# Delta-rule recurrence of a hybrid backbone: Gram products in two halves, the triangular solve woven as a generator

## The chip, the cores and the metric

The kernel runs on one core of one Trainium2 chip. The metric is device time in microseconds (us) of one launch that computes both layers; lower is better. Matrix work is on PE (TensorE; its weight loads are the row PEld), element-wise work on DVE (VectorE) and ACT (ScalarE), small copies on POOL (GpSimd), and SP issues the loads of weights.

## What is computed

The model has two layers over a trunk of 256 context and 512 latent tokens of width 1024. Each layer projects its normed input into three branches (a bidirectional RWKV-7 recurrence, a convolution of 31 taps, grouped-query attention), merges them with gates, and runs a squared-ReLU MLP. The change lies in the recurrence alone, 16 heads of 64 channels, once forward and once in reverse:

```
    def step(S, inp):
        r_t, w_t, k_t, v_t, kk_t, a_t = inp
        s_kk = jnp.einsum('bhij,bhj->bhi', S, kk_t)
        S = (S * w_t[:, :, None, :]
             - s_kk[..., None] * (kk_t * a_t)[:, :, None, :]
             + v_t[..., None] * k_t[:, :, None, :])
        return S, jnp.einsum('bhij,bhj->bhi', S, r_t)
```

The last layer gives out latent tokens only, so that its reads `r` of the context's four chunks of 64 tokens are not needed.

## The kernel before

The recurrence is computed in chunks of 64 tokens, 12 chunks to the 768 tokens, and in pairs of heads: one head lies on partitions 0 to 63, the other on 64 to 127 (`ROWS[0]`, `ROWS[1]`). Eight pairs follow each other in a layer. For one pair the work is, in the order of its data:

- **prep**: the rows `k`, `r`, `v` of the pair come out of the projection; `rw_kk` norms `kk`; `rw_decay` makes the running sums `sg` of the log decay (both directions); `rw_keys` writes `BK`, for each chunk the 128 columns that hold the decayed key and the decayed `kk*a`.
- **grams** (`rw_front`): `KR` takes `kk` (slot 0) and `r` (slot 1), each times the exponential of `sg`. For each of 12 chunks, 2 heads and 2 directions one fp32 matmul has `BK` as stationary operand (64 rows by 128 columns) and both slots of `KR` as moving operand (128 columns; 64 where the last layer needs no `r`). It is issued as two pairs of weight load and matmul in the profile. DVE masks the results into `GL` and `GB`; `GB` takes transposes of `BK` too.
- **seeds and solve** (`rw_seed`, `rw_solve`): DVE inverts the 32x32 triangular blocks of `GL` in some 60 dependent steps between transposes. `rw_rest` meanwhile makes `KM` from `GL`, `UV` and transposes of `KR` slot 0.
- **merge and batch** (`rw_merge`, `rw_batch`): the blocks are joined to 64x64 inverses, and applied.
- **chain** (`rw_chain`): 12 steps, each needs the state `S` of the step before it; it reads `KR`, `GB` and `UV`. Then `rw_readout`.

Beside this run **jobs**: the 128-column slices of the big input projection (line 412), that is `k`, `r` and `v` of the next pair, the convolution's two inputs, and the columns of attention and gates ("spills"). A slice is eight jobs, one for each 128 rows of the contraction, and a job is six matmuls of 384 columns (three of 512 for slices that need latent tokens alone). The 31 **taps** of the convolution run on DVE.

`weave` advances several generators in turn; each yields an estimate in us, and `pe` puts out that many times `ratio` jobs, so that the jobs fill TensorE between the small matmuls. In the kernel before, the loop over pairs weaves merge, batch and chain of pair p with prep and grams of pair p+1 (the grams in three parts, behind `wait('s3')`, `wait('s7')`, `wait('s11')`, which are steps of the chain). Behind that stand `rw_solve`, `rest` and `s.fill(F['solve'])`, 26 jobs in the first layer and 34 in the second. The framework then orders each engine's instructions itself by its own estimate; taps and a few matmuls are pinned. PSUM tiles of the small products come from a pool of two banks (`s.g`).

Of the kernel before, what the change touches and what calls it, by code (L numbers as in the profile page):

```python
# [47 lines left out]
SCHED = [dict(open=1.3, first=0.55, mid=0.5, end=0.4, solve=26, early=4, tap0=1, tap1=1, merge=1.2, sums=0, grams=0, rest=9, ln=9, pad=1, last=1.15, tap2=1),  # L48
         dict(open=1.2, first=0.4, mid=0.4, end=0.4, solve=34, early=5, tap0=0.8, tap1=0.8, merge=1.4, sums=0, grams=0, rest=9, ln=9, pad=1, last=0.85, tap2=1.1)]
# [27 lines left out]
class Kern:  # L77
# [364 lines left out]
    def conv_jobs(s, l, P, j, T, dst):  # L442
# [8 lines left out]
        def done_b(ps):  # L451
            hold['c'] = s.rp.tile([128, L], F32, tag="cv", name="cv")
            nc.scalar.activation(out=s.dv0(hold['c'], T), in_=s.pv(ps, T), func=AF.Tanh, scale=0.5)
# [313 lines left out]
    def rw_keys(s, P, p, I, Q, d):  # L767
# [22 lines left out]
        if d:  # L790
            Q['key', 1] = key
        yield 0.2

    def rw_front(s, I, Q, d, g, lat):

        nc = s.nc
        c = slice(4 * g, 4 * g + 4)
        n = 1 if lat and g == 0 else 2
        sg = s.c64(Q['sg', d])[:, c]
        KR, BK, GL, GB = (s.big[x, d] for x in ('KR', 'BK', 'GL', 'GB'))  # L800

        nc.gpsimd.memset(KR[:, 0, c, 63 * d:63 * d + 1], 1.0)
        nc.scalar.activation(out=KR[:, 0, c, 1 - d:64 - d], in_=sg[:, :, d:63 + d], func=AF.Exp, scale=CDEC)
        nc.scalar.activation(out=KR[:, 1, c], in_=sg, func=AF.Exp, scale=CDEC)
        if ('lam', d) not in Q:
            Q['lam', d] = s.rt("lam%d" % d, [128, 12], 2)
        nc.gpsimd.tensor_copy(Q['lam', d][:, c], KR[:, 1, c, 63 * (1 - d)])
        nc.vector.tensor_tensor(out=KR[:, 0, c], in0=s.c64(I['kk'])[:, c], in1=KR[:, 0, c], op=ALU.mult)  # L808
        if n == 2:
            nc.vector.tensor_tensor(out=KR[:, 1, c], in0=s.c64(I['r'])[:, c], in1=KR[:, 1, c], op=ALU.mult)  # L810
        yield 0.3
        gp = [s.g([128, 4, 2, 64]) for h in range(2)]
        for q in range(4):
            for h in range(2):
                nc.tensor.matmul(gp[h][:, q, 0:n, :], lhsT=BK[ROWS[h], 4 * g + q].rearrange("p a b -> p (a b)"),  # L815
                                 rhs=KR[ROWS[h], 0:n, 4 * g + q, :], start=True, stop=True)
        for h in range(2):
            for x, G in ((0, GL[:, h, c]), (1, GB[:, h, c, 1]))[:n]:
                nc.vector.tensor_tensor(out=G, in0=gp[h][:, :, x, :],
                                        in1=s.mask(d, h, x).unsqueeze(1).to_broadcast([128, 4, 64]), op=ALU.mult)  # L820
        yield 1.0
        bk = s.g([128, 4, 2, 64])
        for q in range(4):
            nc.tensor.transpose(out=bk[:, q].rearrange("p a b -> p (a b)"), in_=BK[:, 4 * g + q].rearrange("p a b -> p (a b)"), identity=s.ident)  # L824
        nc.scalar.activation(out=GB[:, :, c, 0, :], in_=bk.rearrange("p c h j -> p h c j"), func=AF.Copy)
        yield 0.45
# [14 lines left out]
    def rw_rest(s, d):  # L841

        nc = s.nc
        KR, GL, UV, KM = (s.big[x, d] for x in ('KR', 'GL', 'UV', 'KM'))
# [8 lines left out]
        for h in range(2):  # L853
            s.rw_transpose(KR[:, 0].rearrange("p c t -> p (c t)"), h, lambda par: KM[ROWS[h], par::2, 0, :])
            yield 0.35

    def rw_solve(s):
# [5 lines left out]
        for k in range(1, 31):  # L863
# [3 lines left out]
            nc.vector.tensor_tensor(out=X[:, k + 1:, 0:k], in0=X[:, k + 1:, 0:k], in1=tm, op=ALU.add)  # L867
        nc.vector.transpose(out=s.Z[:, 0:1024].rearrange("p (u c) -> p c u", c=32), in_=X.rearrange("p a b -> p b a"))
        nc.vector.transpose(out=s.Z[:, 768:1792].rearrange("p (u t) -> p t u", t=32), in_=X)

    def rw_bonus(s, P, p, I, Q, T):
# [3 lines left out]
        nc.vector.tensor_tensor(out=ks[:, o:], in0=ks[:, o:], in1=Q['key', 1][:, o:], op=ALU.add)  # L875
        nc.vector.scalar_tensor_tensor(out=ks[:, o:], in0=I['r'][:, o:], scalar=P['v']('rw_r_k')[:, p:p + 1], in1=ks[:, o:], op0=ALU.mult, op1=ALU.mult)
        yield 0.1
# [261 lines left out]
    def rwkv_phase(s, l, P, T):  # L1139
# [3 lines left out]
        with ExitStack() as rc:  # L1143
# [31 lines left out]
            def prep(p, I, Q, wait, *held):  # L1175

                return chain(s.after(I, 'k', 0, s.rw_kk(P, p, I)), *held, s.rw_decay(P, p, Q), wait('b0'), s.rw_keys(P, p, I, Q, 0), wait('b1'), s.rw_keys(P, p, I, Q, 1),
                             s.after(I, 'r', 0, s.rw_bonus(P, p, I, Q, T)))

            def grams(I, Q, part):  # L1180

                a, b = ((0, 0), (1, 2), (2, 1))[part]
                c = [slice(0, 8), slice(8, 12)] if part == 1 else [slice(0, 4), slice(8, 12)]
                gs = [s.rw_front(I, Q, 0, a, lat), s.rw_front(I, Q, 1, b, lat)]
                if part == 1:
                    gs.append(s.rw_seed(0, slice(0, 8)))
                if part == 2:
                    gs += [s.rw_seed(1, slice(0, 12)), s.rw_seed(0, slice(8, 12))]
                return chain(*gs)

            def rest(I):
                return chain(s.rw_values(I), s.rw_rest(0), s.rw_rest(1))
            I, In = {}, {}
            s.rw_inputs(l, P, 0, T, I, 'krv')
            s.fill(24)
            Q = s.rw_open(l, 0)
            spills(F['early'])
# [261 lines left out]
```

## Time and profile before

| | |
|---|---|
| median of three runs | 4373.38 us (4372.7 to 4377.01) |
| profiled execution, its own time | 4372.14 us |
| its span, first to last instruction | 4370.4 us |
| mean granted TensorE clock | 0.963 |
| PE busy / PEld busy | 95% / 78% of the span |
| DVE / ACT / POOL busy | 62% / 42% / 7% |
| recurrence of layer 0 / layer 1, steady part | 190 to 1290 us / 2600 to 3540 us |

The span is the time between the first and the last instruction that the trace holds; the execution's own time lies 1.7 us above it, and the median of the three runs 1.2 us above that. Ends of matmuls in the trace are modelled, so that a PE that is shown busy may still be slowed from inside: how long a matmul takes of the engine's time is read from the start of one to the start of what follows it.

### The profile page before, as it was taken

What the parts mean: (1) busy time and instruction counts of PE and PEld (TensorE: products, weight loads), DVE (VectorE), ACT (ScalarE), POOL (GpSimd) and SP (SyncE); (2) the same over time, 40 slices, a digit from 0 to 9 for tenths busy, and PEclk for the clock granted to TensorE, in tenths of its full rate; (3) what the DMA queues carried; (4) which work ended last, traced back from release to release, by engine and by line L of the source; (5) the groups of instructions that cost most, each with busy time, mean ns of one, the idle gap of its engine ahead of it and who ended that gap; (6) DMA issues with size and microseconds to landing.
All of it is one profiled execution on the core that took longest, in us unless ns stands there. A gap on an engine that the chain in (4) does not pass through costs nothing.

```text
span 4370.4 us, 77114 instructions
## 1 busy us (share of the span) xinstructions
PE 4141.8 (95%) x31232; PEld 3410.5 (78%) x31232; DVE 2723.4 (62%) x5238; ACT 1834.4 (42%) x3586; POOL 287.1 (7%) x349
## 2 busy tenths in 40 slices
PE   6999999999998989899999899999999989898998
PEld 4888888888886679689999677887777765575886
DVE  3788888888855554332323577888888855554344
ACT  3444445444534442332223445555545534433332
POOL 0000000000001022200000100000000000121001
PEclk9999999999999999899999889999999979998998
DMA  4212211112134234343322221112221232242332
GB/s 165 78 47 63 64 53 60 51 55 63 59 100 163 69 120 160 110 152 126 102 86 63 72 70 51 58 59 60 66 62 57 73 119 74 65 140 61 97 94 80
DMA packets 443595, 367.73 MB, mean 84 GB/s; under 512 B 19662, under 2 KB 391528, under 8 KB 437096
## 3 DMA queue, kind: packets, MB, share of 16 engines
q1 hardware_dynamic: 422504, 283.10, 21.6%
q10 hardware_dynamic: 20736, 79.70, 5.0%
q8 instruction: 247, 4.05, 0.4%
q14 instruction: 108, 0.88, 0.1%
HBM read 301.38 MB, written 53.48 MB: 81 GB/s over the span
## 4 chain that ended last, share of the span: by engine, by line
PE 80%; DVE 9%; ACT 5%; issue 2%; DMA 2%; POOL 2%; SPq 0%; ACTq 0%; DVEq 0%; POOLq 0%
PE mm L412 31%; PE mm L389 20%; PE g L815 3%; PE g L633 2%; PE g L939 2%; PE sp L960 2%; PE g L928 2%; PE S L612 2%; PE sp L964 1%; PE yp L978 1%; PE yp L976 1%; PE g L850 1%; PE g L1044 1%; PE g L824 1%; PE g L234 1%
## 5 line engine op out<-in xcount | busy, mean ns | idle before, releaser
L328 ACT ACTIVATE wh<-raw 128x512 fp32r<-128x512 f32 x700 | 441.4, 631 | 1249.8 <-PE mm L389 565.5
L332 DVE TENSOR_TENSOR wl<-raw,wh 128x512 fp32r<-128x512 f32 x700 | 502.0, 718 | 697.6 <-ACT wh L328 685.3
L412 PE MATMUL mm<-hh,wh 128*128 128x384 f32 (+1 forms) x2072 | 647.5, 371 | 15.3 <-ACT hh L328 4.8
L412 PE MATMUL mm<-hl,wh 128*128 128x384 f32 (+1 forms) x2072 | 637.9, 367 | 6.1 <-POOL hl L330 6.1
L412 PE MATMUL mm<-hh,wl 128*128 128x384 f32 (+1 forms) x2072 | 634.8, 365 | 0.0
L471 DVE SCALAR_TENSOR_TENSOR cv<-u,dw,cv 128x783 f32<-128x783 f32 (+1 forms) x480 | 426.7, 889 | 2.8
L412 PEld LDWEIGHTS mm<-hh,wh 128*128 128x128 f32 x2072 | 377.6, 192 | 55.1 <-ACT hh L328 7.3
L412 PEld LDWEIGHTS mm<-hl,wh 128*128 128x128 f32 x2072 | 382.6, 192 | 38.0 <-POOL hl L330 8.8
L412 PEld LDWEIGHTS mm<-hh,wl 128*128 128x128 f32 x2072 | 383.0, 192 | 30.5 <-issue 3.2
L412 PE MATMUL mm<-oh,wh 128*128 128x384 f32 (+1 forms) x768 | 252.9, 384 | 9.5 <-DVE acc L1285 6.0
L412 PE MATMUL mm<-ol,wh 128*128 128x384 f32 (+1 forms) x768 | 239.9, 365 | 10.2 <-POOL ol L330 10.2
L389 PE MATMUL mm<-hh,wh 128*128 128x384 f32 (+1 forms) x768 | 239.5, 367 | 5.3 <-ACT hh L347 3.6
L389 PE MATMUL mm<-hl,wh 128*128 128x384 f32 (+1 forms) x768 | 238.3, 365 | 5.1 <-POOL hl L330 4.6
L412 PE MATMUL mm<-oh,wl 128*128 128x384 f32 (+1 forms) x768 | 238.8, 364 | 0.0
L389 PE MATMUL mm<-hh,wl 128*128 128x384 f32 (+1 forms) x768 | 235.8, 362 | 0.0
L389 PE MATMUL mm<-fh,wh 128*128 128x384 f32 (+1 forms) x768 | 229.9, 353 | 0.0
L389 PE MATMUL mm<-fh,wl 128*128 128x384 f32 (+1 forms) x768 | 229.9, 353 | 0.0
L389 PE MATMUL mm<-fl,wh 128*128 128x384 f32 (+1 forms) x768 | 229.5, 352 | 0.0
L815 PEld LDWEIGHTS g<-KR,BK 64*128 64x128 f32 x1536 | 157.3, 204 | 43.0 <-issue 33.7
L815 PE MATMUL g<-KR,BK 64*128 64x128 f32 (+1 forms) x1536 | 178.3, 306 | 5.2 <-DVE KR L808 3.1
L412 PEld LDWEIGHTS mm<-oh,wh 128*128 128x128 f32 x768 | 139.6, 189 | 51.2 <-ACT wh L328 13.6
L966 ACT ACTIVATE S<-sp,lam 128x64 f32<-128x64 f32 x352 | 92.9, 310 | 206.3 <-PE sp L964 199.4
(297 smaller groups left out, 7239.0 us busy)
## 6 DMA issues: line engine op xcount, KB each, us to landing
raw<-in_w_in_dram SPq DMA_DIRECT2D x316, 256.0 KB
raw<-in_w_ff_dram SPq DMA_DIRECT2D x256, 256.0 KB
wmod<-in_w_mod_dram ACTq DMA_DIRECT2D x48, 1024.0 KB
raw<-in_w_branch_dram SPq DMA_DIRECT2D x96, 256.0 KB
z<-f ACTq DMA_DIRECT2D x40, 384.0 KB
gt<-z SPq DMA_DIRECT2D x24, 384.0 KB
raw<-in_w_out_dram SPq DMA_DIRECT2D x32, 256.0 KB
z<-f ACTq DMA_DIRECT2D x32, 256.0 KB
```

Of the source, the lines that this page charges most:

```text
L328: s.last_hi = nc.scalar.activation(out=hi, in_=src, func=AF.Copy)
L332: nc.vector.tensor_tensor(out=lo, in0=src, in1=hi.bitcast(F32), op=ALU.subtract)
L389: nc.tensor.matmul(ps[:, b, :t1 - t0], lhsT=w[:, k % 4, :], rhs=a[:, t0:t1], start=k == 0 and f == 0, stop=k == KT - 1 and f == 2)
L412: s.last_mm = nc.tensor.matmul(s.jps[:, b, :t1 - t0], lhsT=w[:, k % 4, :], rhs=a[:, t0:t1], start=k == 0 and f == 0, stop=k == KT - 1 and ...
L471: s.tap_pin(nc.vector.scalar_tensor_tensor(out=hold['c'], in0=u[:, k:k + L], scalar=w(k), in1=hold['c'], op0=ALU.mult, op1=ALU.add))
L612: nc.tensor.matmul(sps[:, b, :384], lhsT=lq, rhs=kT[kv][:, 384 * b:384 * b + 384], start=True, stop=True)
L633: nc.tensor.matmul(op[:, :nq], lhsT=V[:, kk, kv * 128:kv * 128 + 128], rhs=PT[:, kk, :nq], start=kk == 0, stop=kk == nk // 128 - 1)
L815: nc.tensor.matmul(gp[h][:, q, 0:n, :], lhsT=BK[ROWS[h], 4 * g + q].rearrange("p a b -> p (a b)"), rhs=KR[ROWS[h], 0:n, 4 * g + q, :], sta ...
L928: nc.tensor.matmul(wu[ROWS[h], q - q0], lhsT=TT[ROWS[h], q, :], rhs=KM[ROWS[h], q].rearrange("p a b -> p (a b)"), start=True, stop=True)
L939: nc.tensor.matmul(ap[ROWS[h], q - q0, 0:n, :], lhsT=W[ROWS[h], q, :], rhs=GB[ROWS[h], h, q, 0:n, :], start=True, stop=True)
L960: nc.tensor.matmul(sp[ROWS[h], d], lhsT=GB[d][:, h, q[d], 0, :], rhs=UV[d][:, h * 12 + q[d], :], start=d == 0, stop=d == 1 and k == 0)
L966: nc.scalar.activation(out=Sn[:, d], in_=sp[:, d], func=AF.Copy, scale=Q['lam', d][:, q[d]:q[d] + 1])
```

## The change

The products of `BK` with `kk` and with `r` are taken apart. `rw_rows` computes the decayed `kk` of all 12 chunks in the tiles of `k` and `kk` (one direction each), `rw_rrows` the decayed `r` in the tiles of `sg` and `r`. `rw_lgram` multiplies `BK` with the first alone, eight and then four chunks at a time, `rw_rgram` with the second, four chunks of each direction at a time; ACT copies the decayed `r` into `KR` slot 1 afterwards. Each of these matmuls streams 64 columns where one streamed 128 before. `rw_solve` yields after every second step, and one `weave` holds everything: merge, batch and chain of pair p; prep, KK grams, seeds and solve of pair p+1; its bonus sums and decayed `r`; its R grams and rest. All jobs of a pair are queued at its start, and the ratio is their number over 84.

```
-SCHED = [dict(open=1.3, first=0.55, mid=0.5, end=0.4, solve=26, early=4, tap0=1, tap1=1, merge=1.2, sums=0, grams=0, rest=9, ln=9, pad=1, last=1.15, tap2=1),
+SCHED = [dict(open=1.3, early=4, tap0=1, tap2=0, step=1.0, merge=1.2, sums=0, rest=9, ln=9, pad=1, last=1.15, span=84),
...
-    def rw_front(s, I, Q, d, g, lat):
-        nc.scalar.activation(out=KR[:, 0, c, 1 - d:64 - d], in_=sg[:, :, d:63 + d], func=AF.Exp, scale=CDEC)
-        nc.scalar.activation(out=KR[:, 1, c], in_=sg, func=AF.Exp, scale=CDEC)
...
+    def rw_rows(s, I, Q, lat):
+        for d, e, to in ((0, k, k), (1, s.Z[:, 0:768], kk)):
+            ev, sv = s.c64(e), s.c64(Q['sg', d])
+            nc.gpsimd.memset(ev[:, :, 63 * d:63 * d + 1], 1.0)
+            nc.scalar.activation(out=ev[:, :, 1 - d:64 - d], in_=sv[:, :, d:63 + d], func=AF.Exp, scale=CDEC)
+            nc.vector.tensor_tensor(out=to, in0=kk, in1=e, op=ALU.mult)
+        Q['KK'] = (k, kk)
...
-        for q in range(4):
-            for h in range(2):
-                nc.tensor.matmul(gp[h][:, q, 0:n, :], lhsT=BK[ROWS[h], 4 * g + q].rearrange("p a b -> p (a b)"),
-                                 rhs=KR[ROWS[h], 0:n, 4 * g + q, :], start=True, stop=True)
+    def rw_lgram(s, Q, d, c0, n):
+        gp = [s.g([128, n, 64]) for h in range(2)]
+        for q in range(n):
             for h in range(2):
+                nc.tensor.matmul(gp[h][:, q, :], lhsT=BK[ROWS[h], c0 + q].rearrange("p a b -> p (a b)"), rhs=KK[ROWS[h], c0 + q, :], start=True, stop=True)
         for h in range(2):
+            nc.vector.tensor_tensor(out=GL[:, h, c0:c0 + n], in0=gp[h], in1=s.mask(d, h, 0).unsqueeze(1).to_broadcast([128, n, 64]), op=ALU.mult)
...
+    def rw_rgram(s, Q, part, lat):
+        if part or not lat:
+            gp = [s.g([128, 2, 4, 64]) for h in range(2)]
+            for d in range(2):
+                for q in range(4):
+                    u = cs[d].start + q
+                    for h in range(2):
+                        nc.tensor.matmul(gp[h][:, d, q, :], lhsT=BK[d][ROWS[h], u].rearrange("p a b -> p (a b)"), rhs=R[d][ROWS[h], u, :], start=True, stop=True)
+            for d in range(2):
+                nc.scalar.activation(out=KR[d][:, 1, cs[d]], in_=R[d][:, cs[d]], func=AF.Copy)
...
+            if k % 2 == 0:
+                yield s.sched['step']
...
+            def grams(I, Q, wait):
+                return chain(wait('s3', 'rows'), s.rw_rgram(Q, 0, lat), wait('s7'), s.rw_rgram(Q, 1, lat), wait('s11'), s.rw_rgram(Q, 2, lat),
+                             s.rw_values(I), s.rw_rest(Q, 0), s.rw_rest(Q, 1))
...
                 if more:
-                    gs.append(chain(prep(p + 1, In, Qn, wait, *held), wait('s3'), grams(In, Qn, 0), wait('s7'), grams(In, Qn, 1), wait('s11'), grams(In, Qn, 2)))
+                    gs += stages(p + 1, In, Qn, wait, note, *held)
...
-                s.weave(F['first'] if more else F['last'], *gs)
-                s.taps(len(s.cops))
+                s.weave(len(s.jobs) / F['span'] if more else F['last'], *gs)
                 if more:
-                    s.conv_jobs(l, P, p + 1, T, s.ocv)
...
-                    s.rw_solve()
-                    s.weave(3.0, rest(I))
...
-                    s.fill(F['solve'])
+                    old, I, Q = Q, In, Qn
```

Where the instructions stand is decided by the framework. In the built program of before, these are the grams of a pair in layer 0 on PE; `g` is a PSUM tile, two neighbouring numbers are the two heads of one part (so they lie on different row halves of the array), `mm` is a job, `x2` two matmuls in succession.

```order
L815 MATMUL g_8918<-KR0_673,BK0_672 128x128 x2
L815 MATMUL g_8919<-KR0_673,BK0_672 128x128 x2
L815 MATMUL g_8918<-KR0_673,BK0_672 128x128
L815 MATMUL g_8919<-KR0_673,BK0_672 128x128
L815 MATMUL g_8918<-KR0_673,BK0_672 128x128
L815 MATMUL g_8919<-KR0_673,BK0_672 128x128
L412 MATMUL mm_9222<-hh_145,wl_9213 128x384 x2
L412 MATMUL mm_9222<-hh_145,wh_9212 128x384 x2
L412 MATMUL mm_9222<-hl_146,wh_9212 128x384 x2
L412 MATMUL mm_9222<-hh_145,wl_9213 128x384 x2
L824 MATMUL g_8932<-cst_75,BK0_672 128x128 x4
```

In the changed program the same place of PE reads, behind 16 KK products that alternate between the heads:

```order
L830 MATMUL g_9005<-in_kk_8376,BK1_677 128x64 x4
L412 MATMUL mm_9136<-hh_145,wl_9049 128x384
L830 MATMUL g_9006<-in_kk_8376,BK1_677 128x64 x4
L412 MATMUL mm_9136<-hh_145,wl_9049 128x384
L412 MATMUL mm_9136<-hh_145,wh_9048 128x384 x2
L917 MATMUL g_9023<-key_8832,cst_75 128x384
L830 MATMUL g_9026<-in_k_8273,BK0_672 128x64 x8
L830 MATMUL g_9027<-in_k_8273,BK0_672 128x64 x8
L917 MATMUL g_9064<-key_8832,cst_75 128x384
L412 MATMUL mm_9136<-hl_146,wh_9048 128x384 x2
L412 MATMUL mm_9136<-hh_145,wl_9049 128x384
L847 MATMUL g_9067<-sg_8651,BK0_672 128x64 x4
```

Eight products of 128 columns, in a mixed order of heads, have become products of 64 columns, twice as many, with runs of four and eight for one head. Over the whole program 768 products (640 of 128 columns, 128 of 64) have become 1408 of 64 columns; 508 of the 768 stand in runs of two to four for one head, and 894 of the 1408 in runs of two to eight. In both programs every pair's products stand on PE behind the last step of the chain of the pair before, and ahead of the merge, except one part of the first pairs in the changed one.

On DVE this is the start of a pair's solve in layer 0 before (`GL` and `GB` masks, seeds at line 836, transposes, then steps at lines 866 and 867):

```order
L819 TENSOR_TENSOR GL_679<-g,masks 128x256
L819 TENSOR_TENSOR GB_680<-g,masks 128x4x64
L836 TENSOR_SCALAR Z<-GL_679 32x384 x4
L860 STREAM_TRANSPOSE Z<-Z 128x384
L861 STREAM_TRANSPOSE A<-Z 128x1024
L862 MEMSET A 128x32
L866 TENSOR_TENSOR Z<-A 128x30
L867 TENSOR_TENSOR A<-A,Z 128x30
```

And this is the same place in the changed program (masks of KK at line 832, of R at line 850, steps at lines 899 and 900):

```order
L332 TENSOR_TENSOR wl<-raw,wh 128x512
L832 TENSOR_TENSOR GL_674<-g,masks 128x256 x2
L894 STREAM_TRANSPOSE A<-Z 128x1024
L850 TENSOR_TENSOR GB_675<-g,masks 128x4x64 x2
L850 TENSOR_TENSOR GB_680<-g,masks 128x4x64 x2
L895 MEMSET A 128x32
L899 TENSOR_TENSOR Z<-A 128x30
L332 TENSOR_TENSOR lw<-lraw,lw 128x512
L900 TENSOR_TENSOR A<-A,Z 128x30
L899 TENSOR_TENSOR Z<-A 128x58
```

The solve still follows the last KK mask at once; masks of R have moved into it, and the seeds and the first transpose now stand some rows earlier.

## Rows read from the trace of the kernel before

**Rows 1.** The page: busy us of each engine.

```profile
PE 4141.8 (95%) x31232; PEld 3410.5 (78%) x31232; DVE 2723.4 (62%) x5238; ACT 1834.4 (42%) x3586; POOL 287.1 (7%) x349
```

**Rows 2.** Two stretches, the recurrences: length, busy us by engine, PEclk, DMA.

```profile
190.00:1290.00 1100.00, 1089.40 (x11179) 947.45 (x11179) 907.31 (x1798) 518.79 (x1107) 22.25 (x84) 0.99 0.21 62
2600.00:3540.00 940.00, 921.54 (x9328) 736.10 (x9326) 776.00 (x1635) 482.20 (x1052) 27.34 (x84) 0.97 0.21 63
```

**Rows 3.** What PE waited for, layer 0: us in total, times, longest.

```profile
PE g L901 <- DVE Z L868: 3.4, 3, 1.2
```

**Rows 4.** The same, layer 1.

```profile
PE g L901 <- DVE Z L868: 5.0, 5, 1.2
PE g L882 <- DVE key L876: 4.2, 4, 1.7
PE g L815 <- DVE KR L808: 3.1, 1, 3.1
```

**Rows 5.** One pair, layer 0: chain, grams, solve.

```profile
276.00:303.00 27.00, 27.00 (x323) 22.11 (x324) 21.38 (x28) 14.90 (x39) 2.63 (x10) 1.00 0.10 36
303.00:326.00 23.00, 22.99 (x172) 19.35 (x171) 16.89 (x41) 9.51 (x19) 0.00 (x0) 1.00 0.29 87
326.00:360.00 34.00, 34.00 (x283) 31.39 (x284) 31.30 (x77) 14.06 (x27) 0.00 (x0) 1.00 0.26 70
```

**Rows 6.** Groups on PE, shapes apart: stationary tile, moving tile, count | busy, mean ns.

```profile
L815 PE MATMUL g<-KR,BK 64*128 64x128 f32 x1280 | 138.7, 300 | 2.0 <-ACT GB L825 1.7
...
L815 PE MATMUL g<-KR,BK 64*128 64x64 f32 x256 | 39.5, 336 | 3.2 <-DVE KR L808 3.1
```

**Rows 7.** The same of weight loads.

```profile
L412 PEld LDWEIGHTS mm<-hh,wl 128*128 128x128 f32 x2072 | 383.0, 192 | 30.5 <-issue 3.2 <-DVE GB L819 0.4
...
L815 PEld LDWEIGHTS g<-KR,BK 64*128 64x128 f32 x1536 | 157.3, 204 | 43.0 <-issue 33.7 <-DVE KR L808 3.9 <-ACT GB L825 3.3
...
L928 PEld LDWEIGHTS g<-BK,GL 64*64 64x64 f32 x1536 | 83.0, 134 | 14.1 <-ACT UV L931 5.0 <-issue 4.6 <-ACT y L1019 1.2
```

**Rows 8.** PE in order of time, layer 0: start, us, instructions.

```profile
307.00 1.16 PE L815 MATMUL g<-KR,BK 64*128 64x128 f32 x8
308.08 0.44 PE L412 MATMUL mm<-hl,wh 128*128 128x384 f32 x1
...
319.17 1.56 PE L815 MATMUL g<-KR,BK 64*128 64x128 f32 x16
320.65 0.44 PE L412 MATMUL mm<-hh,wh 128*128 128x384 f32 x1
```

**Rows 9.** PE in order of time, layer 0, another part of that pair.

```profile
311.87 1.16 PE L815 MATMUL g<-KR,BK 64*128 64x128 f32 x16
312.96 0.44 PE L412 MATMUL mm<-hl,wh 128*128 128x384 f32 x1
```

**Rows 10.** PE in order of time, layer 1, part without r.

```profile
2812.44 1.10 PE L815 MATMUL g<-KR,BK 64*128 64x64 f32 x8
2813.47 0.62 PE L412 MATMUL mm<-hl,wh 128*128 128x384 f32 x2
```

**Rows 11.** DVE in order of time: a solve's first and last transposes.

```profile
326.75 0.58 DVE L860 STREAM_TRANSPOSE Z<-Z 128x384 f32<-128x384 f32 x1
...
357.84 2.08 DVE L869 STREAM_TRANSPOSE Z<-A 128x1024 f32<-128x1024 f32 x1
```

**Rows 12.** Two stretches of grams in layer 1.

```profile
2677.00:2695.00 18.00, 17.27 (x74) 14.05 (x74) 9.88 (x24) 4.21 (x8) 0.00 (x0) 0.53 0.27 88
2812.00:2835.00 23.00, 23.00 (x176) 19.62 (x174) 15.05 (x38) 9.53 (x20) 0.00 (x0) 1.00 0.27 84
```

**Rows 13.** DVE in layer 0: a mask of 256 elements, a product of 768.

```profile
L819 DVE TENSOR_TENSOR GL<-g,masks 128x256 f32<-128x256 f32 x84 | 35.3, 420 | 35.6 <-PE g L815 35.2
...
L1008 DVE TENSOR_TENSOR y<-y,st 128x768 f32<-128x768 f32 x7 | 6.7, 957 | 0.2
```

More of the change, by code (lines that the diff above doesn't have):

```diff
@@ L44 @@
 VOFF = {n: 8 * i for i, n in enumerate(VECS)}
-SCHED = [dict(open=1.3, first=0.55, mid=0.5, end=0.4, solve=26, early=4, tap0=1, tap1=1, merge=1.2, sums=0, grams=0, rest=9, ln=9, pad=1, last=1.15, tap2=1),
-         dict(open=1.2, first=0.4, mid=0.4, end=0.4, solve=34, early=5, tap0=0.8, tap1=0.8, merge=1.4, sums=0, grams=0, rest=9, ln=9, pad=1, last=0.85, tap2=1.1)]
+SCHED = [dict(open=1.3, early=4, tap0=1, tap2=0, step=1.0, merge=1.2, sums=0, rest=9, ln=9, pad=1, last=1.15, span=84),
+         dict(open=1.2, early=5, tap0=0.8, tap2=0, step=1.0, merge=1.4, sums=0, rest=9, ln=9, pad=1, last=0.85, span=84)]
 def shape_constants():
@@ L451, in done_b @@
         def done_b(ps):
+            s.taps(len(s.cops))
             hold['c'] = s.rp.tile([128, L], F32, tag="cv", name="cv")
@@ L874, in rw_bonus @@
         ks = bv = Q['key']
-        nc.vector.tensor_tensor(out=ks[:, o:], in0=ks[:, o:], in1=Q['key', 1][:, o:], op=ALU.add)
         nc.vector.scalar_tensor_tensor(out=ks[:, o:], in0=I['r'][:, o:], scalar=P['v']('rw_r_k')[:, p:p + 1], in1=ks[:, o:], op0=ALU.mult, op1=ALU.mult)
+        Q['bonus'] = True
         yield 0.1
@@ L1191, in rest @@
[L1191 to L1197, printed above, removed]
-            s.weave(F['open'], prep(0, I, Q, lambda n: ()))
-            s.conv_jobs(l, P, 0, T, s.ocv)
-            s.weave(F['end'], chain(*(grams(I, Q, k) for k in range(3))))
-            Qn = s.rw_open(l, 1)
-            s.rw_solve()
@@ L1203, in rwkv_phase, with sums @@
-            s.weave(3.0, rest(I))
-            s.rw_inputs(l, P, 1, T, In, 'kr')
-            s.fill(F['solve'])
-            old = None
-            for p in range(8):
-                ev = set()
+                             s.rw_rows(I, Q, lat), *(s.rw_lgram(Q, d, c, n) for d in (1, 0) for c, n in ((0, 8), (8, 4))), wait('rows'),
+                             s.rw_seed(1, slice(0, 12)), s.rw_seed(0, slice(0, 12)))
+            def sums(p, I, Q, wait, note):
+                return chain(wait('keys'), s.after(I, 'r', 0, chain(par(s.rw_bonus(P, p, I, Q, T), chain(s.rw_rrows(I, Q, lat), note('rows'))))))
@@ L1210, in wait, with events @@
+            def events(*ns):
+                ev = set(ns)
                 def wait(*ns):
```

118 lines of the change are left out of this document (73 added, 45 removed).

## The prediction

> **What bounds the kernel now.** I first read the page's busy line [rows 1]: PE 95% of the span, DVE 62%, ACT 42%. That is a mean over very different stages, so I cut out the two recurrences by windows [rows 2]. PE is busy 1089.4 of 1100 us in layer 0 and 921.5 of 940 us in layer 1: 10.6 + 18.5 = 29.1 us of gaps in 2040 us. DVE is next (907 and 776 us), then ACT. Second, what are the gaps? PE's longest total waits are the merge waiting for the solve's last transposes [rows 3, 4], 3.4 and 5.0 us in all, then the bonus sums waiting for `key` (4.2 us) and once for the decayed `kk` (3.1 us). Third, one pair by stage [rows 5]: PE has no gap in the chain (276 to 303), in the grams (303 to 326) nor in the solve (326 to 360), where DVE's dependent steps run 33.2 us from the first transpose to the end of the last [rows 11] under jobs that PE would have to do anyway. So the solve, which looks like a serial stretch in the code, costs PE nothing. What bounds the recurrence is the sum of PE's own time, and a change pays here only by taking time out of PE, or by closing those gaps and the stretches of half clock (granted clock 0.99 and 0.97 of full in the two recurrences [rows 2]).
>
> **What the change adds on PE.** Order and count are read off the two programs, prices off the trace. 768 fp32 products become 1408, each half as wide: the columns streamed are the same, the weight loads are not. How long does a product take of PE? Ends are modelled, so I go from a start to the next start.
>
> - 64 columns, four products of one head (eight instructions): from 2812.44 to 2813.47, 1.03 us [rows 10], that is 0.26 us each.
> - 128 columns, four products of one head: from 307.00 to 308.08, 1.08 us [rows 8], 0.27 us each. Half the columns save 5%.
> - 128 columns, eight products that alternate between the heads: from 311.87 to 312.96, 1.09 us [rows 9], 0.136 us each. The two row halves work side by side.
> - 128 columns, two, two, then four alternating: from 319.17 to 320.65, 1.48 us [rows 8], between the two.
>
> So the price hangs on the order of heads, and hardly on the columns. Why is seen in the loads [rows 7]: a load of 64 rows by 128 columns has a mean of 204 ns, 128 by 128 has 192 ns, 64 by 64 only 134 ns. The columns of the stationary operand set it, and those of the grams remain 128.
>
> The Trainium skill says this too, TensorE: Matmul & The Clock Gate, section LDWEIGHTS (loading the stationary operand): a load's time goes by the stationary operand's columns over 1.2 GHz, whatever its rows, which gives an estimate of 107 ns for 128 columns. By that page the 1280 loads that are added (two to a product) would cost 137 us one after the other, and 68 us if the halves always overlapped. The rows agree in kind (204 against 134 ns), and the sum below does not use it.
>
> The check of my prices on the kernel before: 508 products in runs x 0.27 + 260 alternating x 0.136 = 172 us, against 138.7 + 39.5 = 178.2 us busy [rows 6], some of it at half clock. Of the changed program: 894 in runs x 0.26 + 514 alternating x 0.136 = 302 us. The difference is 130 us. In runs of eight the entry into the run is paid once instead of twice. Taking 1.03 us as 0.9 of steady work and 0.13 of entry (0.9 is what 1.48 and 1.09 us allow: runs of two plus alternating ones add up with 0.225 and 0.11 us a product), the difference is 894 x 0.225 + 514 x 0.11 - (508 x 0.225 + 260 x 0.11) = 115 us. I take the middle, **+122 us**. From below: no row shows products of 64 columns that alternate; at half of the 0.136 us, 514 of them would cost 35 us less, so +90 us. From above: +130 us. Layer 0 has 384 added products of the 640, so it bears about three fifths.
>
> **What the change moves.** On PE nothing gets beside the chain: products of the next pair stand behind its last step before and after, in all pairs but the first. What does move is that KK's masks, seeds and solve no longer wait for R's masks, and that R's grams and masks lie under the solve, where by count about 20 jobs remain of about 30 (the rest have gone between the steps ahead). By count PE still has about as much under the solve as DVE needs for it: fewer jobs, but the R products have come instead. Cost nothing, covered by this; if the cover fell short, the merge would wait at the place that waits now, whose longest wait is 1.2 us: 16 pairs x 1.2 = 19 us as the upper bound, nothing as the lower; I take 0 because the framework balanced both.
>
> **What it removes.** Gaps and half clock: at most 29.1 us of gaps, and 0.01 x 1100 + 0.03 x 940 = 39 us of clock, 68 us in all. Nothing guarantees either, and some gaps (the first pair, bonus sums) remain in the code; the waits that the edit can touch are those of the merge, of `key` and of the decayed `kk`, 3.4 + 5.0 + 4.2 + 3.1 = 15.7 us. I take **-22 us**, these and a little clock; bounds 0 and -68.
>
> **What costs nothing.** On DVE 192 masks of 256 elements become 64 of 256 and 64 of 512, and 176 products of 256 become 48 of 768 and 16 of 512 [rows 13]; with 0.42 us a short one and 0.96 us a long one DVE saves some 25 us of 1683. On ACT 192 short exponentials become 64 long ones and 80 copies into `KR`, on POOL 128 instructions go. The jobs on PE cover all this. POOL's large wait for the chain in `rw_front` was never PE's. DMA is the same: 1110 rows on SP in both programs. The jobs are the same in number, and the changes between jobs and small products on PE too (by count 2113 in the two recurrences before, 2052 after).
>
> **The sum.** 4372.1 us (the profiled execution) + 122 - 22 = 4472 us. The median of the runs lies 1.2 us above that execution, within the sum's own uncertainty.
>
> **The rivals.**
>
> *A. Products of 64 columns cost half.* Then PE's sum does not grow, the decoupled masks close gaps, and the kernel gets faster: 4372 - 22 to - 68, about 4330 us. It decides from the point where a product of 64 columns takes less than about 0.14 us in the mix of the new order (172 + 22 us over 1408 products). For it: the columns streamed are equal in sum. Against it: 1.03 against 1.08 us [rows 8, 10], the same shape on the same array. The Trainium skill, same page, section Back-to-back issue gap, gives for a lone matmul N / 2.4 plus some 2.5 ns, by which 64 columns take half of 128; the same section warns that a stream with loads is set by both. The rows side with the loads.
>
> *B. The clock or the cover gives way as well.* In layer 1 a stretch of grams ran at a mean clock of 0.53 (2677 to 2695) where the next pair's ran at 1.00 [rows 12]; PE ahead of it had waited 3.1 us for `kk` [rows 4]. The new grams are longer, with fewer jobs among them. 18 us at 0.53 cost 18 x 0.47 = 8.5 us; in each of layer 1's eight pairs that is 68 us, and with the 19 us of merge waits 4372 + 122 + 87 = 4581 us, or half of that, 4537.
> Against it: PE has work queued throughout, and most pairs before kept the clock.
>
> *C. Cheap alternation and all gaps closed.* +90 - 68 gives 4394 us, slower by 0.5%. It needs both ends at once.
>
> *D. The recurrence is not PE's sum after all*, because busy PE hides waits, and the added loads sink into them. Then the time would stay within some us of 4372. Against it: in windows of the chain, the grams and the solve alike PE's starts follow each other without a hole [rows 5].
>
> **How the numbers follow.** Forecast (4420 to 4510) 0.62; B (4510 to 4590) 0.17; C (4385 to 4420) 0.10; D 0.04; A 0.07. A measurement of this kernel can tell about 0.2%, 9 us, from no change. So slower 0.89, same 0.04, faster 0.07. The range of 8 in 10 takes the forecast, most of C's upper half and the lower part of B: 4410 to 4530 us.
>
> **What would show it.** In the profile of the changed kernel: lines 830 and 847 together have 2816 matmul instructions and about 295 us busy where line 815 had 178 [rows 6]; a run of eight products of one head takes about 1.9 us from start to next start; the two recurrences are longer by about 70 and 40 us, and everything outside is unchanged; PE is still busy over 98% there, with the merge's wait for the last transposes at 10 us or less. Wrong would be: runs of 64 columns at half of 0.26 us (A); a granted clock under 0.95 in layer 1, or the merge's wait over 20 us (B); recurrences of unchanged length with PE busier in them (D).

## The result: slower by 4.4%, and the profile after

The changed kernel takes 4569.14 us (median of four runs, 4548.45 to 4581.7) where the kernel before, on the same chip, took 4375.03: ratio 1.0439, 95% interval 1.0399 to 1.0479. The forecast was 4472 us, with a range of 4410 to 4530: the sign was right, the size was short by about 97 us. The profiled execution took 4581.7 us, the longest of the four, with a span of 4579.9, so that 209.5 us of span have to be accounted for. The page's busy line stands against [rows 1]:

```profile
PE 4346.8 (95%) x32512; PEld 3601.1 (79%) x32512; DVE 2719.8 (59%) x5062; ACT 1838.2 (40%) x3474; POOL 255.3 (6%) x221
```

PE grew by 205 us, DVE and ACT did not. The two recurrences by windows, with the ends moved to the same places in the program as in [rows 2]:

```profile
190.00:1392.00 1202.00, 1192.74 (x11917) 1038.18 (x11916) 917.57 (x1724) 526.33 (x1075) 11.61 (x28) 0.95 0.19 57
2710.00:3757.00 1047.00, 1007.10 (x9902) 816.46 (x9897) 778.89 (x1586) 489.58 (x1009) 9.29 (x28) 0.91 0.19 56
```

They are longer by 102 and 107 us, and the rest of the program hardly changed. Two columns differ from [rows 2] in a way that the sum did not have: the granted clock is 0.95 and 0.91 instead of 0.99 and 0.97, and in layer 1 PE is busy only 96.2%. PE's waits (us in all, times, longest) show what it was waiting for, against [rows 3, 4]:

```profile
PE g L830 <- DVE in_kk L803: 31.3, 8, 7.3
...
PE g L936 <- DVE Z L903: 9.9, 13, 1.1
```

The merge's wait for the solve stayed small. New is a wait of the KK products for the decayed `kk`, 29.1 of the 31.3 us in layer 1. The groups of the gram lines, against [rows 6]:

```profile
L830 PE MATMUL g<-in_k,BK 64*128 64x64 f32 x768 | 121.2, 348 | 0.0
L847 PE MATMUL g<-sg,BK 64*128 64x64 f32 x640 | 95.0, 332 | 0.0
L847 PE MATMUL g<-in_r,BK 64*128 64x64 f32 x640 | 88.2, 329 | 0.0
L830 PE MATMUL g<-in_kk,BK 64*128 64x64 f32 x768 | 83.0, 323 | 32.4 <-DVE in_kk L803 31.3 <-DVE GL L832 1.1
```

2816 instructions as counted, but 387 us busy instead of the 295 forecast. One pair of layer 0 (pair 2) shows where they go; PE in order of time, against [rows 8, 9]:

```profile
477.10 2.00 PE L830 MATMUL g<-in_kk,BK 64*128 64x64 f32 x32
479.03 0.44 PE L412 MATMUL mm<-hh,wh 128*128 128x384 f32 x1
...
480.44 1.10 PE L830 MATMUL g<-in_kk,BK 64*128 64x64 f32 x8
481.48 0.44 PE L412 MATMUL mm<-hl,wh 128*128 128x384 f32 x1
...
484.24 3.39 PE L830 MATMUL g<-in_k,BK 64*128 64x64 f32 x32
487.56 1.06 PE L917 MATMUL g<-key,cst 128*128 128x384 f32 x2
...
503.51 2.24 PE L847 MATMUL g<-sg,BK 64*128 64x64 f32 x13
...
508.03 1.01 PE L412 MATMUL mm<-hh,wh 128*128 128x384 f32 x2
...
512.73 1.17 PE L847 MATMUL g<-sg,BK 64*128 64x64 f32 x13
...
515.06 0.62 PE L412 MATMUL mm<-hh,wl 128*128 128x384 f32 x2
```

From start to next start, 16 products that alternate take 1.93 us, 16 in two runs of one head 3.32 us, four of one head 1.04 us. The last two groups are the same 16 R products in the same order: 4.52 us the first time, 2.33 us the second. Between them only the clock differs, and PE has no gap. The windows over that pair's grams, and over pair 4's:

```profile
477.00:515.00 38.00, 38.00 (x252) 34.16 (x251) 18.87 (x41) 9.06 (x18) 0.00 (x0) 0.69 0.13 42
796.00:824.00 28.00, 27.73 (x254) 24.60 (x254) 19.14 (x43) 9.85 (x19) 0.00 (x0) 1.00 0.23 73
```

254 instructions against 252, 10 us apart: pair 4 kept the full clock, pair 2 spent 24 us at half. The clock fell there at 488 us, behind the runs of one head and with PE busy all the time, and rose at 512, between the two groups of R products. Before the change this stretch took 20 us in pair 1 (304 to 324) at clock 1.00.

I summed over all PE instructions of both traces the time from a start to the next start, without idle time ("half" is how much of it lay at the half level, 1.2 GHz):

```
                                before      after       change   half
products of BK with kk and r    171.1       343.2       +172     35 -> 193
jobs (L412)                     1822        1877        +55      73 -> 162
transposes of BK                42          53          +12      9 -> 31
chain's products (S, UV, KR)    282         255         -27      20 -> 17
everything else                                         -7
idle time of PE                                         +4
                                                        +209
```

If time at half level is counted half, the grams' own growth is +93 us (the loads), and half clock adds 79 us in the grams, 44 in the jobs and 11 in the transposes; the other products had a little less of it than before. Over all of PE half clock costs 127 us more: **about 130 us of the 209**. The other terms come to -11 us. Since this execution lies 12.6 us above the median, the clock's share of the median's 194 us is rather less, an estimate of 115 us: the four executions' mean granted clocks, 0.938 to 0.945, put 34 us of lost clock between the longest and the shortest, whose times are 33 us apart.

### The profile page after: what moved, and what is told of

Its sections match the earlier page's. It is cut to its first block, busy times and chain, and to the rows that moved or that the text cites. A ratio compares the mean times of both kernels' runs of the same rounds, so it can differ in the third digit from the quotient of the medians.

```text
span 4579.9 us, 79160 instructions
## 1 busy us (share of the span) xinstructions
PE 4346.8 (95%) x32512; PEld 3601.1 (79%) x32512; DVE 2719.8 (59%) x5062; ACT 1838.2 (40%) x3474; POOL 255.3 (6%) x221
## 5 line engine op out<-in xcount | busy, mean ns | idle before, releaser
L412 PE MATMUL mm<-hh,wh 128*128 128x384 f32 (+1 forms) x2072 | 671.4, 384 | 13.2 <-ACT hh L347 4.0
L412 PE MATMUL mm<-hh,wl 128*128 128x384 f32 (+1 forms) x2072 | 648.8, 372 | 0.9 <-DVE wl L332 0.9
L412 PEld LDWEIGHTS mm<-hh,wh 128*128 128x128 f32 x2072 | 377.8, 196 | 66.0 <-issue 11.3
L412 PEld LDWEIGHTS mm<-hl,wh 128*128 128x128 f32 x2072 | 391.8, 195 | 38.2 <-POOL hl L330 8.8
L412 PEld LDWEIGHTS mm<-hh,wl 128*128 128x128 f32 x2072 | 393.5, 196 | 32.2 <-issue 4.4
L389 PE MATMUL mm<-hh,wh 128*128 128x384 f32 (+1 forms) x768 | 238.0, 365 | 6.4 <-ACT hh L347 3.6
L389 PE MATMUL mm<-hh,wl 128*128 128x384 f32 (+1 forms) x768 | 234.8, 360 | 0.0
L389 PEld LDWEIGHTS mm<-hh,wh 128*128 128x128 f32 x768 | 141.5, 191 | 37.7 <-ACT wh L328 15.9
L900 DVE TENSOR_TENSOR A<-A,Z 128x30 f32<-128x30 f32 (+14 forms) x480 | 158.9, 331 | 12.9
```

What stands on the lines that cost most here:

```text
L389: nc.tensor.matmul(ps[:, b, :t1 - t0], lhsT=w[:, k % 4, :], rhs=a[:, t0:t1], start=k == 0 and f == 0, stop=k == KT - 1 and f == 2)
L412: s.last_mm = nc.tensor.matmul(s.jps[:, b, :t1 - t0], lhsT=w[:, k % 4, :], rhs=a[:, t0:t1], start=k == 0 and f == 0, stop=k == KT - 1 and ...
```

## The experiments

The table gives, from first to last gram of a layer, the length and the time at half clock in it (summed over the clock's records in the trace), and the ratio to the kernel before on the same chip.

```
kernel               median    ratio [95%]                L0 us / half   L1 us / half
before               4375      1                          1016 /  12     913 /  66
after                4569      1.0439 [1.0399, 1.0479]    1124 / 147    1018 / 215
e1_split             4499      1.0297 [1.0272, 1.0322]    1074 /  54     995 / 173
e2_weave             4415      1.0105 [1.0082, 1.0128]    1004 /   0     978 / 191
e3_after_alt         4444      1.0166 [1.0143, 1.0190]    1054 /  20     958 / 106
e4_before_alt        4415      1.0111 [1.0081, 1.0142]    1028 /  19     955 / 138
e5_after_jobs        4521      1.0328 [1.0291, 1.0366]    1088 /  82    1005 / 208
e6_after_taps        4627      1.0567 [1.0541, 1.0593]    1104 / 106    1075 / 287
e7_weave_layer0      4353      0.9953 [0.9937, 0.9968]    1004 /   0     912 /  64
e8_after_alt_taps    4506      1.0303 [1.0285, 1.0320]    1049 /  10    1012 / 176
e9_alt_kk            4463      1.0215 [1.0200, 1.0229]    1058 /  24     961 / 105
e10_alt_r            4517      1.0325 [1.0303, 1.0346]    1093 /  85    1016 / 228
e11_layer0_first     4369      0.9993 [0.9982, 1.0005]    1015 /  31     927 /  97
e12_layer0_taps      4346      0.9944 [0.9932, 0.9956]    1005 /   7     897 /  70
e13_late_kk          4457      1.0201 [1.0184, 1.0218]    1074 /  14     958 / 106
e14_alt_rows         4404      1.0072 [1.0053, 1.0090]    1049 /  10     927 /  79
```

My theory at the start was the prediction's (the loads, priced by the order of heads); rivals were the weave itself, and later the clock (C) and the wait that starts it (W).

### The two halves of the change apart

e1 splits the products of the kernel before, nothing else:

```
-nc.tensor.matmul(gp[h][:, q, 0:n, :], ..., rhs=KR[ROWS[h], 0:n, 4 * g + q, :], ...)
+for x in range(n):
+    nc.tensor.matmul(gp[h][:, q, x, :], ..., rhs=KR[ROWS[h], x, 4 * g + q, :], ...)
```

> The kernel before, with nothing changed but that each gram product of 128 columns is issued as two of 64 columns with the same stationary tile, so 1408 products instead of 768, and 1364 of them in runs for one head. Theory L (the added weight loads cost PE time, at 0.225 us a product in a run, and the stretches of grams they lengthen lose the clock): slower than before by 1364 x 0.225 + 44 x 0.11 - 143 = 169 us at full clock and more with the clock lost, 4540 to 4660 us. Theory W (the single weave, that is the new order of jobs, solve and rest, is what costs, and the split is nearly free): 4370 to 4400 us.

e2 takes the single weave with the solve as a generator, the grams as before:

```
+            if k % 2 == 0:
+                yield s.sched['step']
...
+return [chain(prep(...), wait('s3'), grams(I, Q, 0), ..., grams(I, Q, 2), note('g'), solve()), chain(wait('g'), rest(I))]
```

> The other half alone: the single weave of the change (solve as a generator, all jobs of a pair queued at its start, ratio by 84, taps flushed at the convolution's input), but the grams as before, 768 products of 128 columns from KR. Theory L: within 30 us of the kernel before, 4345 to 4405 us, with about as much half clock as before in the recurrences. Theory W: slower by most of the 194 us, 4500 us or more.

The split costs 131 us: the added loads cost, and rival A is out. In the sum over starts its grams grow by 107 us, 74 when half time is counted half; the rest is clock. That is less than expected (169 us at full clock, 4540 us or more in all): 0.16 us a product on the mean, though 1364 of the 1408 stand in runs. So products in runs have no single price. Sixteen of e1's take 2.33 us in the group shown and 3.10 in the one ahead of it, where two runs of eight of the changed kernel took 3.32:

```profile
470.99 2.40 PE L816 MATMUL g<-KR,BK 64*128 64x64 f32 x32
473.32 0.44 PE L412 MATMUL mm<-hh,wl 128*128 128x384 f32 x1
```

How long e1's runs are is not on record. The weave costs 47 us, which I did not expect, and not evenly: layer 0 is 12 us shorter, layer 1 is 65 us longer. Its layer 1 waits of PE:

```profile
PE mm L412 <- DVE wl L332: 31.4, 5, 12.0
PE g L885 <- DVE key L879: 21.5, 4, 11.1
```

DVE is late there, and half clock rose from 66 to 191 us; in e1's layer 1 it rose to 173. 131 + 47 = 178 us, against 194 for the whole change, but the halves do not add up layer by layer, and the near sum is luck. In layer 0 they give 58 - 12 = 46 us where the whole change costs 108, in layer 1 82 + 65 = 147 where it costs 105. The half clock of layer 0 (147 us, against 54 and 0) comes with the two halves together.

### The order of heads

e3 chains the matmuls of the changed kernel so that heads alternate; e4 does so in the kernel before:

```
+m = nc.tensor.matmul(...)
+if q or h:
+    s.behind(m, last)
+last = m
```

> The changed kernel, with the products of a part chained in issue order so that the two heads always alternate (1408 products alternating, none in a run; by count about 58 job matmuls instead of 39 then lie among a pair's grams in layer 0, 40 instead of 20 in layer 1). Theory L: a product falls from 0.225 to about 0.11 us, 894 of them, so 100 us less at full clock, and the stretches get short and dense enough to keep more of the clock: 4400 to 4470 us. Theory W: no gain, 4540 us or more.

> The kernel before with the same chaining of heads in its 768 products of 128 columns; nothing else. If a product's price hangs on the order of heads as the rows of before showed (0.27 us in a run, 0.136 us alternating), 508 products get cheaper by 0.115 to 0.134 us: 58 to 68 us less, 4305 to 4320 us, and it beats both kernels. If PE was not the bound there, no change: 4365 to 4385 us.

By the ratios e3 gave back 119 us (0.0273 of 4371), and the price law can be read off it, PE in order of time:

```profile
309.55 0.43 PE L830 MATMUL g<-in_kk,BK 64*128 64x64 f32 x2
309.91 0.44 PE L412 MATMUL mm<-hh,wh 128*128 128x384 f32 x1
...
310.62 1.10 PE L830 MATMUL g<-in_kk,BK 64*128 64x64 f32 x14
311.65 0.62 PE L412 MATMUL mm<-hh,wl 128*128 128x384 f32 x2
...
2998.04 0.69 PE L830 MATMUL g<-in_kk,BK 64*128 64x64 f32 x2
2998.66 0.79 PE L412 MATMUL mm<-hl,wh 128*128 128x512 f32 x1
```

One product takes 0.36 us, seven take 1.03: 0.25 for the entry and 0.112 for each. At half clock one takes 0.62 us. But only about 45 of the 119 us are price (93 to 48 us of full-clock growth, where 100 us were expected): half clock in layer 0 fell from 147 to 20 us and in layer 1 from 215 to 106.

e4 was a miss: slower by 1.1% where 4305 to 4320 us were expected. The order became one product, jobs, then seven, so the entry was paid twice:

```profile
312.20 0.48 PE L815 MATMUL g<-KR,BK 64*128 64x128 f32 x2
312.62 0.45 PE L412 MATMUL mm<-hh,wl 128*128 128x384 f32 x1
...
313.35 1.16 PE L815 MATMUL g<-KR,BK 64*128 64x128 f32 x14
314.44 0.63 PE L412 MATMUL mm<-hl,wh 128*128 128x384 f32 x2
```

0.42 + 1.09 = 1.51 us for eight against 1.60 on the mean before, at full clock; over all grams 15 us were saved. Against that the jobs cost 31 us more, PE's idle time is 17 us longer, and layer 1 has 138 us at half clock instead of 66. Why it lost the clock there is not settled.

e9 and e10 alternate KK alone and R alone:

> The changed kernel with its KK products alone alternating between the heads (980 products alternate, 428 lie in runs of one head, where the changed kernel has 514 and 894). Alternation of both kinds took the time from 4569 to 4444 us and half clock in the two recurrences from about 360 to 126 us. In the changed kernel's layer 0 half clock begins 10 to 18 us into a pair's grams, behind the KK product runs of one head. Theory K (the runs of KK start it): half clock in layer 0 falls under 40 us, ratio to before about 1.022, 4470 us. Theory KR (any run of one head counts alike, so each kind bears its share): about half of the gain, 4505 us, half clock in layer 0 at 60 to 90 us. Layer 1 keeps the wait for the decayed kk, about 30 us, in either case.

> The changed kernel with its R products alone alternating between the heads (940 products alternate, 468 in runs). Theory K (the runs of KK start the half clock): half clock in layer 0 stays above 90 us and the time falls by the price of the R products alone, 426 products x about 0.1 us = 40 us at the most, to 4530 to 4550 us. Theory KR: about half of alternation's gain, 4505 us, half clock in layer 0 at 60 to 90 us.

KK alone gives 98 of the 119 us and leaves 24 us of half clock in layer 0, as theory K said. R alone gives 50 us and leaves 85 us, between the two theories by its time. But these totals do not tell K from KR. Of e10's 85 us, 44 lie in pair 0, where PE waits ahead of the grams (2.2 us). In pairs 1 to 7, where it does not, these are the pairs that fall to half clock, the time at half in them, and the job matmuls among a pair's grams (e5, e6, e8, e13 and e14 follow below):

```
                                  pairs      half us     jobs
after; e6, the same layer 0       6; 5 of 7  113; 72     35 to 45
e5, more jobs, same order         6 of 7     75          69 to 90
e9, KK alternates                 3 of 7     24          47 to 54
e10, R alternates                 3 of 7     34          44 to 59
e3, e8, e13, e14, all alternate   0 of 28    0           56 to 71
e1, loop of before, split         2 of 7     20          30 to 43
```

So in layer 0 either kind's runs keep about half of the falls, and only without both are there none. Alternation also brought more jobs between the products; e5 has still more of them and falls all the same, so it is the order of heads and not the jobs. Runs alone do not settle it either: e1 has most of its products in runs and falls in two pairs only; how long its runs are would have to be known. What KK alone gives beyond R lies to a good part in layer 1 (105 us at half against 228), where the KK products are the first behind a wait. The gains overlap (98 + 50 is more than 119).

### The clock with the order kept

e5 puts more jobs among the grams:

```
-        yield 0.2 * n
+        yield 0.5 * n
...
-            yield 1.4
+            yield 3.5
...
-... step=1.0 ...
+... step=0.4 ...
```

> The changed kernel with more jobs among the grams and fewer beside the solve's steps (yields of the KK grams 0.2 to 0.5 a chunk, of the R grams 1.4 to 3.5, of a solve step 1.0 to 0.4): by count some 68 to 104 job matmuls among layer 0's 96 products of a pair where the changed kernel has 34 to 44, in layer 1 15 to 28 (one pair 74) where it has 15 to 34. Loads, products and the order of heads stay. Theory C (half clock among the grams is what the changed kernel pays beyond the price of the loads): half clock inside layer 0's recurrence falls from about 147 us to under 60, layer 1 hardly changes, and the time falls by about 0.45 x 90 = 40 us, to about 4525 us (ratio to before about 1.035). Theory L (the loads alone): no change, 4569 us within 10. Rival S (the solve loses its cover): the merge's wait for Z, 9.9 us, grows to 40 us or more and the time stays or rises, up to 4600 us.

48 us faster with the same loads in much the same order, half clock in layer 0 down to 82 us (expected: under 60), in layer 1 hardly changed (208 us). The merge's wait stayed at 8.9 us, so S is out. C holds by the time. That jobs among the grams keep the clock is shown for pair 0 alone (0 us at half instead of 34, with 105 jobs instead of 40): in pairs 1 to 7 the 75 us lie within what two executions of the changed order had (113 and 72).

### The wait

e6 moves layer 1's taps behind the KK products; e8 does the same with alternating heads:

```
-... early=5, tap0=0.8, tap2=0, ...
+... early=5, tap0=0.25, tap2=0.8, ...
```

> The changed kernel with layer 1's taps moved: tap0 0.8 to 0.25, tap2 0 to 0.8, so that about 10 instead of 21 to 30 taps of a pair stand on DVE ahead of the second product of rw_rows and some 21 beside the solve. At 0.65 us a tap DVE is about 13 us earlier there. Theory W (PE's wait for the decayed kk, 31.3 us in all, also starts the half clock of layer 1's grams): the wait falls to under 6 us, half clock in layer 1's recurrence from about 215 to about 120 us, and the time by 28 + 0.45 x 95 = 70 us, to about 4500 us. Theory C (the half clock comes from the stream of short products itself, wait or no wait): half clock stays at about 200 us, the time falls by the wait alone, to about 4540 us. Rival S: the taps get between the solve's steps, the merge waits 40 us or more, and little or nothing is won.

> The changed kernel with its grams alternating between the heads, as in the earlier experiment (ratio 1.0166, about 126 us of half clock in the recurrences), and layer 1's taps moved as in the run with taps (tap0 0.25, tap2 0.8). Theories C and W together: the wait for the decayed kk falls from 33.8 to under 6 us, half clock to about 75 us, and the time from 4444 to about 4395 us, ratio 1.006. It stays above the kernel before by the price of the loads at full clock, which 640 added products at 0.11 to 0.13 us put at 70 to 80 us against what the alternation itself saves. If the wait is replaced by one of the merge for the solve: 4440 us or more.

Both became slower by about 60 us, rival S (a tap of 512 columns takes 0.75 us in the trace, not 0.65). The kk wait of e6's layer 1 fell to 3.6 us, but its waits now begin with the following rows, beside the solve and the taps' buffer:

```profile
PE mm L412 <- ACT cv L454: 72.2, 4, 19.0
PE g L936 <- DVE Z L903: 46.3, 8, 18.0
```

Pair by pair they still tell something. In e6, seven pairs of layer 1 have no wait ahead of the grams, and five of these fall to half clock 11 or 12 us into the grams. In e8, with alternating heads, the same seven pairs have none at all; its 176 us at half lie outside of them. And layer 0 of e6 is the very program of layer 0 of the changed kernel: 1104 us with 106 at half against 1124 with 147, so a microsecond at half costs 19.4/41.0 = 0.47 us. The pair that took 38 us above took 27 here:

```profile
479.00:506.00 27.00, 27.00 (x252) 24.02 (x250) 18.26 (x39) 8.81 (x18) 0.00 (x0) 1.00 0.18 60
```

e13 and e14 both start from e3: e14 covers the wait with jobs and leaves the taps,

```
         Q['KK'] = (k, kk)
-        yield 0.4
+        yield 8.0 if lat else 0.4
```

> The same alternating kernel with a yield of 8.0 instead of 0.4 behind rw_rows in layer 1, so that jobs can stand between the rows and the KK grams; the taps stay. If PE's wait for the decayed kk (33.8 us in all) is covered by these jobs, theory W has half clock in layer 1's grams fall from about 80 us to under 30 and the time by 30 + 25 us, to about 4390 us, ratio 1.005. If the framework puts the jobs elsewhere, the wait and the half clock stay, ratio 1.0166.

and e13 tries to put such a wait into layer 0:

```
         k, kk, o = I['k'], I['kk'], CTX if lat else 0
+        for _ in range(0 if lat else 8):
+            nc.vector.tensor_scalar(out=kk, in0=kk, scalar1=1.0, scalar2=None, op0=ALU.mult)
```

> The changed kernel with alternating heads (ratio 1.0166; in its layer 0 PE does not wait ahead of the grams of pairs 1 to 7 and no half clock lies in them) with one thing added: in layer 0 DVE multiplies kk by 1.0 eight times in place ahead of the products of rw_rows, so that the decayed kk comes some 4 to 8 us later in each pair. Products, loads, order of heads and, within 10, the jobs among the grams stay as they are. Theory W (a wait of PE ahead of the grams starts half clock in them, even with alternating heads): PE waits 1 us or more ahead of the grams in most pairs of layer 0, and each of these has 7 to 20 us of half clock in its grams; with 3 us of waiting and 6 us for the clock in each pair the time rises by up to 70 us. Theory H (the order of heads alone decides it, the wait only costs itself): the waits appear, the grams of layer 0 keep the full clock, and the time rises by the waits alone, 10 to 40 us. If other work covers the delay, there is neither.

e13 tells nothing on W: other work covered the delay, PE did not wait in layer 0. e14 does. Its kk wait in layer 1 is 12.0 us where e3 has 31.7, and the time falls by 41 us. First two of its pairs, without and with the wait (4.5 us), then e3's pair that corresponds to the first (7.3 us of wait):

```profile
2961.00:2987.00 26.00, 25.70 (x219) 19.45 (x218) 18.05 (x40) 10.27 (x20) 0.00 (x0) 1.00 0.27 81
3344.00:3375.00 31.00, 30.84 (x217) 23.57 (x217) 19.81 (x44) 10.06 (x19) 0.00 (x0) 0.80 0.24 69
```

```profile
2992.00:3021.00 29.00, 28.97 (x218) 22.45 (x219) 19.91 (x44) 10.44 (x20) 0.00 (x0) 0.87 0.27 82
```

All four pairs of e14's layer 1 with a wait of 2.8 to 4.5 us ahead of the grams have 7 to 14 us at half in them, and the other four, with 0.6 us or less, have none. After such a wait the first grams thus run at half clock even with alternating heads. A shorter wait does not always do it: ahead of the first grams of layer 0 PE waits 1.9 to 2.2 us in eight of the kernels (the changed one, e3, e5, e6, e8, e9, e10, e14), and half clock follows in six, not in e5 and e9.

### A version that is faster than both

e7 has e2's weave in layer 0 and the loop of before in layer 1 (`if l == 0:` ... `else:`); e11 and e12 vary its layer 1 (`first=0.5, solve=28`; `tap0=0.5`):

> The single weave with the solve as a generator in layer 0 alone, with the grams as before; layer 1 has the loop of the kernel before. The experiment with the weave in both layers lost 47 us, but its layer 0 was 14 us shorter from first to last gram and had no half clock there, while layer 1 was longer with about 190 us of half clock. If the layers are independent: 4368 - 14, about 4355 us, ratio 0.997, layer 1 as before. If what was won in layer 0 had only been moved to what follows it: 4368, ratio 1.000. If the weave costs in layer 0 too: 4385 or more.

> The weave in layer 0 alone (ratio 0.9953) with more jobs beside layer 1's chain (first 0.4 to 0.5) and fewer beside its solve (34 to 28). In layer 1 of that kernel PE waits 11 us for key in five places and about 64 us of the recurrence are at half clock, where a wait stood ahead of the grams in most pairs. If jobs ahead of the grams take the place of these waits: 11 us and 0.45 x 40 = 18 us less, 4325 us, ratio 0.989. If the order ahead of the grams hardly moves (by count the jobs among the grams stay at 16 to 18): 4353 us, 0.995. If the solve loses its cover: 4380 us, the merge's wait over 40 us.

> The weave in layer 0 alone (ratio 0.9953) with layer 1's taps slowed (tap0 0.8 to 0.5), so that fewer taps stand on DVE ahead of key and KR and the rest come ahead of the solve. If the wait ahead of the grams starts their half clock here as in the changed kernel: the 11 us of waits for key and some 40 us of half clock go, 4325 us, ratio 0.989. If the taps only move in front of the solve, the merge waits for Z 40 us or more: 4380 us or more.

```profile
166.00:1169.00 1003.00, 985.91 (x10221) 856.60 (x10223) 847.34 (x1680) 482.51 (x1034) 31.54 (x84) 1.00 0.20 59
2532.00:3444.00 912.00, 895.49 (x8867) 715.35 (x8867) 745.92 (x1572) 466.28 (x1011) 27.14 (x84) 0.96 0.20 60
```

e7's two recurrences: layer 0 is 12 us shorter, layer 1 as before. It is 0.5% faster than the kernel before. e11 and e12 both missed the 0.989 hoped for. e12 (0.9944) cannot be told from e7: layer 1 lost 15 us, the waits for `key` went from 11.1 to 6.9 us, and the half clock stayed. e11 lost the gain: the waits for `key` went from 11 to 17 us.

## Why the prediction was wrong, step by step

- **PE bounds the recurrences, and added loads cost.** Right: e1 alone makes the kernel 3.0% slower at an equal number of streamed columns.
- **The price, +122 us.** The order of heads sets it, but the size was off: +93 us at full clock, just inside the lower bound of 90. A run of eight of one head takes 1.66 us, not 1.9. What I split into 0.225 us a product and 0.13 of entry is nearer to 0.19 and 0.28 (1.04 us for four, 3.32 for sixteen): a quarter of the time of my runs of four was entry. The split did not fit its own rows either: with 0.11 us a product it gives 1.01 us for eight that alternate, and the row says 1.09. By the same prices e1 was to add 169 us, and it added 74. The guess that alternating products of 64 columns might be cheaper was wrong: seven take 1.03 us, seven of 128 columns 1.09.
- **"Cost nothing" and the clock: the step that failed.** The sum had a gain of a little clock and no loss; the measured term is about +130 us. The reason given against rival B was that PE has work queued throughout and most pairs kept the clock. The first half did not hold in layer 1, where PE came to wait (next point). The second half was true only of the old stream: in layer 0 the changed kernel drops to half level with PE's row full, in 6 of the 7 pairs without a wait, and in none once all heads alternate (e3, e8, e13, e14). Why pairs of one and the same order fall in one execution and not in another stays open. B's own price, 68 us, counted layer 1 alone; layer 0 carries 135 of the 284 us of added half time. That B's full sum, 4581 us, meets the profiled 4581.7 is luck: the 19 us of merge waits in it did not come, and its clock term was half of the measured one.
- **The cover of the solve.** Right: the merge waits 9.9 us. But a wait came that I had not priced: in layer 1 the decayed `kk` of all twelve chunks is late on DVE, 29.1 us in seven waits, and behind such waits the grams run at half clock (e14).
- **-22 us of gaps closed.** What came is about half, and by other means: idle time did not fall (+4 us), since the new wait replaced the old ones, while the chain's own products became 27 us cheaper, which I had not seen. Jobs cost about 11 us more at full clock; I had them at nothing. With the rest that makes -11 us, within my bounds by luck.
- **What would show it.** The recurrences grew by 102 and 107 instead of 70 and 40 us; a clock under 0.95 in layer 1 was named as the mark of B, and it reads 0.91. The time lies in the range that was given to B with a chance of 0.17.

On the loads, the Trainium skill, TensorE: Matmul & The Clock Gate, section LDWEIGHTS (loading the stationary operand), gives columns over 1.2 GHz, an estimate of 107 ns for 128 columns, so 0.107 us a product of two loads if the loads of the two row halves overlap and 0.213 if they do not. The trace comes near at full clock: 0.112 alternating, about 0.19 in long runs, a tenth below that estimate. At half clock it does not: 16 R products took 4.52 instead of 2.33 us.

## What to carry to other kernels

When a change makes small products more numerous, price the clock as well as the loads: here each microsecond of a busy PE at half clock cost 0.47 us, in the jobs between the products too. Let successive small products lie on different row halves, and give PE something to do just ahead of them. But measure it: the same alternation made the kernel before 1.1% slower (e4), and more jobs among the products alone did not keep the clock in most pairs (e5). Before merging stages, look at which layer has slack on the helper engine: the same weave gained 12 us in layer 0 and lost 65 in layer 1, where DVE was late.

## Unexpected of the hardware

Half clock came with no idle time of PE ahead of it (pair 2 above). It also varied between executions of one program: the same layer 0 had 147 and 106 us of it, and the same pair took 38 and 27 us. The changed kernel's four runs spread over 33 us, as far as their mean clocks do (0.938 to 0.945). Those of the kernel before spread over 4 us on that chip, but over 18 and 21 us on two others, where more were taken.
